# The norm ahead of the MLP: per chunk half, beside the second half of the output projection, in a region of fixed order

## The chip, the core and the metric

The kernel runs on one core of a Trainium2 chip. The metric is device time in microseconds (us) of one execution. Engines are named as the profile names them: PE (TensorE), DVE (VectorE), ACT (ScalarE), POOL (GpSimd), and SP, whose queue issues most DMAs. PE's clock has two levels here, 1.2 and 2.4 GHz; the profile gives the granted one as a share of the higher.

## The reference, cut to what matters

```python
    mixed = jnp.concatenate([rmsnorm(attn, g_attn_out), rmsnorm(ssm, g_ssm_out)], axis=-1) @ w_out
    h = x + mixed
    hn = rmsnorm(h, g_mlp)
    h = h + jnp.square(jax.nn.relu(hn @ w_up)) @ w_down
```

There are 1088 token columns, a model width of 1024 and an MLP width of 4096. All is in 32-bit floats; the kernel gets there by splitting each operand of a product in a high and a low part and adding three products (high by high, high by low, low by high).

## The kernel before

**Layout.** Tokens lie along columns. The 1088 columns fall into two halves `t` (544 each), and each half into two chunks `c` of `NC` = 272. `hp[c][t]` (128 x 8 x 272) holds `h` of one such quarter, in eight groups of 128 rows.

**The second half of the output projection.** `wo_part(w, zh, zl, c, t, mp)` makes two of the eight row groups of one quarter by 24 matmuls of 272 columns and adds them onto `hp[c][t]` on DVE (L1511). The attention half of `w_out` runs first; the state-space half (`wo2`) is the loop of 16 parts ahead of `Top, rrs = {}, {}`: four parts `mp` for each quarter, in the order c0t0, c0t1, c1t0, c1t1.

**The norm.** `norm_sq` squares a quarter on ACT and adds the squares up on POOL (t = 0) or DVE (t = 1); `mlp_norm(c)` begins when both quarters of a chunk are done. It sums over partitions by eight matmuls with a column of ones (L1622), makes the reciprocal root in a chain of small DVE and ACT operations (`rsqrt_col`, L84 to L92), spreads it over the partitions by eight transposes (L1633), copies the rows to SBUF, and multiplies `hp` by gain and rows (L333, 128x272 each).

**The MLP's operands.** The first product, `hn @ w_up`, is done block by block with seven products instead of eight (Strassen and Winograd's scheme). Its seven operands of a chunk, `Hop[c][0..6]` (`ho` in the rows), are blocks of `hn` or sums and differences of them (`nt`), each split in high (ACT cast, L1670) and low (DVE subtraction, L51), 128x1088 each. On the weights' side `w_stream` loads a set of 512 KB blocks (`wr`), forms the sums (`ws`, DVE, 128x512) and splits each of the seven in high (ACT, L1595) and low (POOL, L51): tiles `wl`, six buffers.

**The order of products.** `up_pair(0)` does the sets 0 and 1 for chunk 0 alone (14 products of 12 matmuls; results in `hold`), so that PE has work while chunk 1 is normed. Then `up_set(b)` does set 2 to 15 for both chunks (14 products each), `up_pair(1)` does sets 0 and 1 for chunk 1, and the second product of the MLP follows. The names on PE's rows are `Xp`, `Yp`, `Zp` in a pair and `X`, `Y`, `Z` in a set; a set makes X, Y, X, Y, X, Z, X.

**What sets the order.** `mlp_norm` is a generator: `pump()` runs each live one to its next `yield` after every part or product. The order in which the code then stands is not the order on the engines: outside of `tc.manual_schedule()` the framework's scheduler orders each engine's instructions by its own estimate and by which buffer is free. Inside it, an engine keeps the order of the code. Each engine works through its own queue in that order, and an instruction that waits holds up all behind it. PSUM gives four buffers of 128 x 2 x 512 (`psa`); pages (`pg`, 15 of them) hold `hp`, the projection's operands and weights, and `ho`.

Of the kernel before, what the change touches and what calls it, by code (L numbers as in the profile page):

```python
# [22 lines left out]
EPS = 1e-6  # L23
# [6 lines left out]
def tile_hybrid_step(ctx: ExitStack, tc: tile.TileContext, I: dict, O: dict):  # L30
# [1467 lines left out]
    def wo_part(w, zh, zl_, c, t, mp):  # L1498

        c0 = NH * t + NC * c  # L1500
        ps = psa(f"pw{c}{t}_{mp}")
        for k in range(2):
            m_ = slice(128 * (2 * mp + k), 128 * (2 * mp + k) + 128)
            o = ps[:, k, :NC]
            for kt in range(4):
                rh, rl = zh[kt // 2][:, kt % 2, c0:c0 + NC], zl_[kt // 2][:, kt % 2, c0:c0 + NC]
                pe.matmul(o, lhsT=w[kt][0][:, m_], rhs=rh, start=(kt == 0), stop=False)  # L1507
                pe.matmul(o, lhsT=w[kt][0][:, m_], rhs=rl, start=False, stop=False)  # L1508
                pe.matmul(o, lhsT=w[kt][1][:, m_], rhs=rh, start=False, stop=(kt == 3))  # L1509
        o = hp[c][t][:, 2 * mp:2 * mp + 2]  # L1510
        dve.tensor_tensor(o, ps[:, :, :NC], o, op=ALU.add)  # L1511
        pump()
# [3 lines left out]
    wo_part(wo, ah, al, *order[0])  # L1516
# [24 lines left out]
    for c, t, mp in order[1:2]:  # L1541
        wo_part(wo, ah, al, c, t, mp)
    live.append(ssm_norm())
    for c, t, mp in order[2:]:
        wo_part(wo, ah, al, c, t, mp)
# [14 lines left out]
    def w_stream():  # L1560
# [54 lines left out]
    Hop = [[], []]  # L1615

    def sums(sq, name):

        ps = psb(name + "s")
        for t in range(2):  # L1620
            for j in range(4):
                pe.matmul(ps[:TT, 4 * t + j:4 * t + j + 1], lhsT=sq[:, t, TT * j:TT * j + TT], rhs=ones,  # L1622
                          start=True, stop=True)
        return ps

    def inv_rows(ps, name):

        rsqrt_col(col[0][:TT], ps[:TT, 0:8], 1024, [t[:TT] for t in col[1:3]])
        yield
        pr_ = psa(name + "r")  # L1630
        for t in range(2):
            for j in range(4):
                pe.transpose(pr_[:, t, TT * j:TT * j + TT], col[0][:TT, 4 * t + j:4 * t + j + 1].to_broadcast([TT, 128]),  # L1633
                             ident[:TT, :TT])
        rows = rq([128, 2, NC], name + "rows")
        act.copy(rows, pr_[:, :, :NC])
        return rows

    nsq = []

    def norm_sq(c, t, mp, part):

        if mp == 1:
            part[c, t] = rq([128, 4, NC], f"ns{c}{t}a")
            act.activation(part[c, t], hp[c][t][:, 0:4], AF.Square)
        elif mp == 3:
            s1, s2 = part[c, t], rq([128, 4, NC], f"ns{c}{t}b")
            act.activation(s2, hp[c][t][:, 4:8], AF.Square)
            e = dve if t else pool
            e.tensor_tensor(s1, s1, s2, op=ALU.add)  # L1650
            e.tensor_tensor(s1[:, 0:2], s1[:, 0:2], s1[:, 2:4], op=ALU.add)
            e.tensor_tensor(nsq[c][:, t], s1[:, 0], s1[:, 1], op=ALU.add)
            c0 = NH * t + NC * c
            nc.sync.dma_start(hs[:, :, c0:c0 + NC], hp[c][t])

    def mlp_norm(c):

        sq = nsq[c]
        rows = yield from inv_rows(sums(sq, f"n{c}"), f"n{c}")
        yield  # L1660

        def quarter(k, t):
            for kt in range(4 * k, 4 * k + 4):
                z = hp[c][t][:, kt]
                stt(z, z, g_ml[:, kt:kt + 1], rows[:, t], ALU.mult, ALU.mult)
            return hp[c][t][:, 4 * k:4 * k + 4]

        def operand(src, le):
            h = pg([128, 2, 4, NC], f"ho{c}_{len(Hop[c])}", F32R)
            act.copy(h[:, 0], src)  # L1670
            lo_sub(le, h[:, 1], src, f(h[:, 0]))
            Hop[c].append(h)

        b11 = quarter(0, 0)
        operand(b11, dve)
        yield
        b12 = quarter(0, 1)
        t1 = rq([128, 4, NC], f"nt1{c}")
        dve.tensor_tensor(t1, b12, b11, op=ALU.subtract)
        operand(t1, dve)  # L1680
        yield
        b22 = quarter(1, 1)
        t2 = rq([128, 4, NC], f"nt2{c}")
        dve.tensor_tensor(t2, b22, t1, op=ALU.subtract)
        operand(t2, dve)
        yield
        t3 = rq([128, 4, NC], f"nt3{c}")
        dve.tensor_tensor(t3, b22, b12, op=ALU.subtract)
        operand(b22, dve)
        yield  # L1690
        operand(t3, dve)
        yield
        b21 = quarter(1, 0)
        operand(b21, dve)
        yield
        dve.tensor_tensor(t2, b21, t2, op=ALU.subtract)
        operand(t2, dve)
# [13 lines left out]
    def relu2(z):  # L1711
        stt(z, z, 0.0, z, ALU.max, ALU.mult)

    def up_evac(i, o, z):

        if i in (0, 1, 2):
            act.copy(z(*((0, 0), (1, 1), (1, 0))[i]), o)
        elif i in (3, 4, 5):
            z = z(*((1, 0), (1, 1), (0, 0))[i - 3])
            dve.tensor_tensor(z, o, z, op=ALU.add)  # L1720
            relu2(z)
        else:
# [21 lines left out]

    for _ in range(4):
        ahead.append(next(wst))
    part = {}
    for c in range(2):
        nsq.append(rq([128, 2, NC], f"nsq{c}"))
        for t in range(2):  # L1750
            for mp in range(4):
                wo_part(wo2, sh, sl, c, t, mp)
                norm_sq(c, t, mp, part)
        live.append(mlp_norm(c))
# [28 lines left out]

    def up_pair(c):

        rt = [hold[:, s_] if c == 0 else rq([128, 2, 2, NC], f"rb{s_}") for s_ in range(2)]
        made = {}
        for i, x in enumerate(SEQ):
# [3 lines left out]
            for s_ in range(2):  # L1792
                w = w_next()
                while len(Hop[c]) <= i:
                    pump()
                o = made[x][:, s_, :NC]
                up_product(w, o, i, c, first)
                up_evac(i, o, lambda k, q: rt[s_][:, k, q])
            pump()
            if c == 1 and 1 <= i < 5:  # L1800
# [3 lines left out]
    def up_set(b):  # L1804
        rt = [rq([128, 2, NH], f"r{x}{b}") for x in "ab"]
        made = {}
        for i, x in enumerate(SEQ):
            w = w_next()
# [3 lines left out]
            for c in range(2):  # L1812
                while len(Hop[c]) <= i:
                    pump()
                up_product(w, made[x][:, c, :NC], i, c, first)
            up_evac(i, made[x][:, :, :NC], lambda k, q: rt[k][:, q].rearrange("p (c n) -> p c n", c=2))
            pump()
# [3 lines left out]
    up_pair(0)  # L1821
    for b in range(2, 16):
# [40 lines left out]
    for g in range(8):  # L1863
        for jp in range(2):
# [3 lines left out]
            for i, x in enumerate(SEQ):  # L1868
                w = w_next()
# [19 lines left out]
    ws = [w_next() for _ in range(7)]  # L1889
# [322 lines left out]
```

## Time and profile before

| | us |
|---|---|
| runs: 1386.16, 1387.05, 1392.28; median | 1387.05 |
| the profiled execution, its own time | 1385.12 |
| its span, first to last instruction | 1382.9 |
| PE busy in it | 1299.2 (94%) |
| DVE, POOL, ACT busy | 1039.1, 685.6, 662.5 |

PE is busy for 94% of the span. Its clock is granted in full nearly everywhere (0.980 in the mean). In the 40 slices of the page, each 34.6 us long, slices 19 to 21, where the projection's second half ends and the MLP begins, are among those with PE busy for less than nine tenths.

### The profile page before, as it was taken

How to read it: one execution, taken by the hardware profiler on the slowest of the kernel's cores; microseconds unless marked ns; L12 is line 12 of the kernel's file. 1: busy time of each engine (PE TensorE's matmuls, PEld its weight loads, DVE VectorE, ACT ScalarE, POOL GpSimd, SP SyncE). 2: the span in 40 equal slices, each digit the busy share in tenths (PEclk: the TensorE clock that was granted, in tenths of full speed). 3: DMA queues.
4: the chain of work that ended last, by engine and by line, in shares of the span. 5: the costliest groups of instructions: out<-in, count | busy, mean ns of one | idle time of the engine just before them, and what ended most of it. 6: DMA issues, size and time to landing. Idle time of an engine off the chain costs nothing.

```text
span 1382.9 us, 24883 instructions
## 1 busy us (share of the span) xinstructions
PE 1299.2 (94%) x9552; PEld 1258.4 (91%) x9552; DVE 1039.1 (75%) x1658; ACT 662.5 (48%) x1325; POOL 685.6 (50%) x646
## 2 busy tenths in 40 slices
PE   7999998989999997998599999999989999999996
PEld 6999997978888887998599999999979999999996
DVE  8679779876888766659877557565699778888756
ACT  6576677655788762224232232332446333343333
POOL 3647656341535426243465455455547455453554
PEclk9999999999999999999899999999999999999998
DMA  5111111210233234132233353342668445654103
GB/s 220 64 41 41 35 35 36 77 48 8 48 76 78 69 94 128 31 126 69 71 129 128 135 175 115 147 167 104 207 235 295 134 154 161 202 163 140 62 1 130
DMA packets 81286, 151.38 MB, mean 109 GB/s; under 512 B 10128, under 2 KB 28816, under 8 KB 81168
## 3 DMA queue, kind: packets, MB, share of 16 engines
q1 hardware_dynamic: 76464, 144.78, 32.7%
q10 hardware_dynamic: 4704, 5.01, 1.1%
q8 instruction: 76, 1.25, 0.4%
q14 instruction: 42, 0.34, 0.1%
HBM read 98.66 MB, written 41.40 MB: 101 GB/s over the span
## 4 chain that ended last, share of the span: by engine, by line
PE 46%; DVE 9%; POOL 3%; issue 2%; DMA 2%; ACT 1%; SPq 0%; DVEq 0%; POOLq 0%; ACTq 0%
PE dX L1701 4%; PE dX L1702 4%; PE dX L1703 4%; PE X L1701 3%; PE X L1703 3%; PE X L1702 3%; POOL wl L51 2%; PE dY L1701 2%; PE dY L1703 2%; PE dY L1702 2%; PE pw L1507 2%; PE pw L1508 2%; PE pw L1509 2%; PE Y L1701 2%; PE Y L1703 2%
## 5 line engine op out<-in xcount | busy, mean ns | idle before, releaser
L51 POOL TENSOR_TENSOR wl<-ws,wl 128x512 fp32r<-128x512 f32 x101 | 163.4, 1619 | 237.0 <-ACT wl L1595 234.8
L51 POOL TENSOR_TENSOR wl<-wr,wl 128x512 fp32r<-128x512 f32 x135 | 210.7, 1569 | 105.6 <-ACT wl L1595 102.4
L1595 ACT CAST wl<-ws 128x512 fp32r<-128x512 f32 x102 | 63.3, 621 | 194.0 <-DVE ws L1583 85.6
L1701 PE MATMUL dX<-to,wl 128*128 128x272 f32 x512 | 149.3, 292 | 2.1 <-DVE q L1858 1.4
L1702 PE MATMUL dX<-to,wl 128*128 128x272 f32 x512 | 148.1, 289 | 0.0
L1703 PE MATMUL dX<-to,wl 128*128 128x272 f32 x512 | 147.6, 289 | 0.0
L1703 PE MATMUL X<-ho,wl 128*128 128x272 f32 x448 | 129.5, 290 | 5.4 <-POOL wl L51 5.4
L1701 PE MATMUL X<-ho,wl 128*128 128x272 f32 x448 | 128.4, 291 | 2.0 <-DVE rb L1720 2.0
L1702 PE MATMUL X<-ho,wl 128*128 128x272 f32 x448 | 128.8, 289 | 0.0
L1595 ACT CAST wl<-wr 128x512 fp32r<-128x512 f32 x136 | 83.9, 620 | 90.4 <-PE dX L1703 31.6
L1581 DVE TENSOR_TENSOR ws<-wr,wr 128x512 f32<-128x512 f32 x34 | 30.8, 905 | 103.2 <-DMA wr<-in_w_up_dram 79.2
L1701 PEld LDWEIGHTS dX<-to,wl 128*128 128x128 f32 x512 | 97.2, 190 | 3.1 <-issue 1.1
L1702 PEld LDWEIGHTS dX<-to,wl 128*128 128x128 f32 x512 | 97.1, 190 | 0.0
L1703 PEld LDWEIGHTS dX<-to,wl 128*128 128x128 f32 x512 | 96.9, 189 | 0.0
L1858 DVE TENSOR_TENSOR q<-dX,q 128x544 f32<-128x544 f32 x108 | 76.0, 717 | 27.8 <-PE dX L1703 27.6
L1703 PEld LDWEIGHTS X<-ho,wl 128*128 128x128 f32 x448 | 84.6, 189 | 5.9 <-POOL wl L51 5.9
L1701 PEld LDWEIGHTS X<-ho,wl 128*128 128x128 f32 x448 | 83.9, 189 | 2.4 <-DVE rb L1720 2.4
L1702 PEld LDWEIGHTS X<-ho,wl 128*128 128x128 f32 x448 | 84.6, 189 | 0.0
L51 DVE TENSOR_TENSOR to<-rr,to 128x1088 fp32r<-128x1088 f32 x56 | 83.5, 1496 | 1.3 <-ACT to L1776 1.3
L1701 PE MATMUL dY<-to,wl 128*128 128x272 f32 x256 | 74.7, 292 | 4.7 <-DVE rb L333 3.1
L1703 PE MATMUL dY<-to,wl 128*128 128x272 f32 x256 | 74.5, 291 | 1.6 <-POOL wl L51 1.6
L1702 PE MATMUL dY<-to,wl 128*128 128x272 f32 x256 | 74.3, 290 | 0.0
(707 smaller groups left out, 4653.6 us busy)
## 6 DMA issues: line engine op xcount, KB each, us to landing
rr<-rd SPq DMA_DIRECT2D x56, 544.0 KB, 5.0
wr<-in_w_up_dram SPq DMA_DIRECT2D x36, 512.0 KB, 4.4
wr<-in_w_dn_dram SPq DMA_DIRECT2D x32, 512.0 KB, 4.7
rd<-rc SPq DMA_DIRECT2D x16, 544.0 KB, 3.6
rd<-re SPq DMA_DIRECT2D x16, 544.0 KB, 3.7
rd<-ra SPq DMA_DIRECT2D x28, 272.0 KB, 3.1
xw<-in_x_dram SPq DMA_DIRECT2D x8, 544.0 KB, 6.8
hp<-in_x_dram ACTq DMA_DIRECT2D x4, 1088.0 KB, 6.1
```

Source lines behind the costliest of these rows:

```text
L51: eng.tensor_tensor(out, src, hi, op=ALU.subtract)
L1507: pe.matmul(o, lhsT=w[kt][0][:, m_], rhs=rh, start=(kt == 0), stop=False)
L1508: pe.matmul(o, lhsT=w[kt][0][:, m_], rhs=rl, start=False, stop=False)
L1509: pe.matmul(o, lhsT=w[kt][1][:, m_], rhs=rh, start=False, stop=(kt == 3))
L1581: dve.tensor_tensor(s_, a21, a22, op=ALU.add)
L1595: act.copy(w[:, 0], src)
L1701: pe.matmul(o, lhsT=lh, rhs=rh, start=first, stop=False, skip_group_check=True)
L1702: pe.matmul(o, lhsT=lh, rhs=rl, start=False, stop=False, skip_group_check=True)
L1703: pe.matmul(o, lhsT=ll, rhs=rh, start=False, stop=last, skip_group_check=True)
L1858: dve.tensor_tensor(z, o[:, :, :NC], z, op=ALU.add)
```

## The change

The 16 parts of the projection's second half, the norm, sets 0 and 1 for chunk 0 and the whole of set 2 now stand in one `tc.manual_schedule()` region. `mlp_norm(c, t)` is a generator for one quarter: it begins after the third part of its own quarter and works beside the parts that follow. Its sums and transposes are four and four; the rows stay in PSUM and the multiplications read them there; all sums of squares are on DVE; each operand's low part is put off to the next step (`later`). `up_pair(0)` is replaced by `up_first`: chunk 0 goes through sets 0 and 1 by eight plain products for each set (24 matmuls for each of eight weight tiles, 192 in all, where the pair had 168), which need the four plain blocks of chunk 0 (`ho0_0`, `ho0_7`, `ho0_5`, `ho0_3`) and eight plain weight tiles, whose low parts are made on DVE (not POOL) and need no sums. Evacuation of `up_first` and of set 2's squared ReLU is on ACT. The operands 1, 2, 4 and 6 of chunk 0 are first needed in set 2. Before and behind the region the order on the engines is that of before but for a few instructions.

```diff
+        load(0)
+        yield
         for j, ns in enumerate(SETS):
             load(j)
+            if j == 0:
+                for n, raw in zip(ns, raws[j]):
+                    for q in range(4):
+                        w = wo4([128, 2, 512], f"wl{j}_{n}_{q}", F32R)
+                        act.copy(w[:, 0], raw[q % 2][:, q // 2])
+                        lo_sub(dve, w[:, 1], raw[q % 2][:, q // 2], f(w[:, 0]))
+                        if n == ns[0] and q == 3:
+                            load(1)
+                        yield w
+                del raws[j]
+                continue
...
+    def mlp_norm(c, t):
+        x, hc = hp[c][t], Hop[c]
+        s1, s2 = (rq([128, 4, NC], f"ns{c}{t}{k}") for k in range(2))
+        act.activation(s1, x[:, 0:4], AF.Square)
+        yield
+        yield
+        act.activation(s2, x[:, 4:8], AF.Square)
...
+        dve.tensor_tensor(s1, s1, s2, op=ALU.add)
+        dve.tensor_tensor(s1[:, 0:2], s1[:, 0:2], s1[:, 2:4], op=ALU.add)
+        dve.tensor_tensor(s1[:, 0], s1[:, 0], s1[:, 1], op=ALU.add)
+        yield
+        for _ in range(c + (c and t)):
+            yield
+        ps = psa(f"n{c}{t}")
+        for j in range(4):
+            pe.matmul(ps[:TT, 1, j:j + 1], lhsT=s1[:, 0, TT * j:TT * j + TT], rhs=ones, start=True, stop=True)
...
+        for j in range(4):
+            pe.transpose(ps[:, 0, TT * j:TT * j + TT], col[c][:TT, 4 * t + j:4 * t + j + 1].to_broadcast([TT, 128]),
+                         ident[:TT, :TT])
+        yield
+        def scale(k):
             for kt in range(4 * k, 4 * k + 4):
+                z = x[:, kt]
+                stt(z, z, g_ml[:, kt:kt + 1], ps[:, 0, :NC], ALU.mult, ALU.mult)
...
+    def up_first():
...
+                o = psa(f"d{s_}{r}")
+                for k in range(2):
+                    w = ahead.pop(0)
+                    for t in range(2):
+                        up_product(w, o[:, t, :NC], ((0, 7), (5, 3))[k][t], 0, k == 0)
+                    flush()
+                    w_next()
+                    step()
...
+    with tc.manual_schedule():
+        next(wst)
+        for n, (c, t) in enumerate(parts):
+            for mp in range(4):
+                late.append(wo_part(wo2, sh, sl, c, t, mp))
+                if len(late) > 1:
+                    late.pop(0)()
+                if mp == 2:
+                    live.append(mlp_norm(c, t))
+                step()
+                if 4 * n + mp in WAT:
+                    w_next()
+        up_first()
+        up_set(2, True)
+    for b in range(3, 16):
+        up_set(b)
```

On PE, where the norm's sums (`n1s`) and transposes (`n1r`) of chunk 1 stood before, among the products of the first pair:

```order
L1703 MATMUL Xp0_7489<-ho0_0_7308,wl0_0_0_6958 128x272
L1622 MATMUL n1s_7528<-ones_67,nsq1_7197 68x1 x4
L1701 MATMUL Yp0_7543<-ho0_1_7343,wl0_0_1_6965 128x272
...
L1703 MATMUL Yp0_7543<-ho0_3_7415,wl0_1_3_7562 128x272
L1633 MATMUL n1r_7578<-ident_64,col0_6944 128x68 x8
L1701 MATMUL Zp0_7720<-ho0_5_7479,wl0_0_5_7634 128x272
```

And PE now, for the two quarters of chunk 1 (`n10`, `n11`; `pw11_3` is the last part of the projection, `d00` to `d11` are `up_first`):

```order
L1668 MATMUL n10_7449<-ones_67,ns100_7322 68x1 x4
L1507 MATMUL pw11_3_7463<-sh0_6421,wo4_6785 128x272
...
L1680 MATMUL n10_7449<-ident_64,col1_6945 128x68 x4
L1737 MATMUL d00_7496<-ho0_0_7273,wl0_0_0_7133 128x272
...
L1668 MATMUL n11_7639<-ones_67,ns110_7460 68x1 x4
L1737 MATMUL d10_7650<-ho0_0_7273,wl0_1_0_7286 128x272
...
L1680 MATMUL n11_7639<-ident_64,col1_6945 128x68 x4
L1737 MATMUL d11_7722<-ho0_0_7273,wl0_1_2_7561 128x272
```

The sums of chunk 1's first quarter have moved ahead of the projection's last part, its transposes behind it, and those of the second quarter stand 96 and 144 matmuls into `up_first`; set 2 follows `d11`.

On DVE, ahead of chunk 1's sums before (`ns11a`, `nsq1` are the sums of squares of the last quarter, `ho0` the operands of chunk 0):

```order
L51 TENSOR_TENSOR ho0_2_7384<-nt20_7382,ho0_2_7384 128x1088
L51 TENSOR_TENSOR ho0_3_7415<-hp01_6134,ho0_3_7415 128x1088
L1696 TENSOR_TENSOR nt20_7382<-hp00_6133,nt20_7382 128x1088
L51 TENSOR_TENSOR ho0_4_7446<-nt30_7413,ho0_4_7446 128x1088
L51 TENSOR_TENSOR ho0_5_7479<-hp00_6133,ho0_5_7479 128x1088
L1650 TENSOR_TENSOR ns11a_7418<-ns11a_7418,ns11b_7482 128x1088
L51 TENSOR_TENSOR ho0_6_7525<-nt20_7382,ho0_6_7525 128x1088
L1651 TENSOR_TENSOR ns11a_7418<-ns11a_7418 128x544
L1652 TENSOR_TENSOR nsq1_7197<-ns11a_7418 128x272
```

And DVE now, the end of the chain from the last quarter's reciprocal root (L1670 to L333) to `ho1_1`, the second operand of chunk 1:

```order
L1728 TENSOR_TENSOR nt01_7446<-hp01_6134 128x1088
L51 TENSOR_TENSOR ho1_0_7603<-hp10_6135,ho1_0_7603 128x1088
L1731 TENSOR_TENSOR nt02_7447<-hp00_6133,nt02_7447 128x1088
L1670 TENSOR_SCALAR n11_7639<-n11_7639 68x4
...
L51 TENSOR_TENSOR ho0_4_7634<-nt01_7446,ho0_4_7634 128x1088
L51 TENSOR_TENSOR ho1_5_7637<-hp10_6135,ho1_5_7637 128x1088
...
L333 SCALAR_TENSOR_TENSOR hp11_6136<-hp11_6136,gains_65,n11_7639 128x272 x4
L1713 TENSOR_TENSOR nt11_7809<-hp11_6136,hp10_6135 128x1088
L1722 TENSOR_TENSOR nt12_7810<-hp11_6136,nt11_7809 128x1088
L51 TENSOR_TENSOR ho1_1_7824<-nt11_7809,ho1_1_7824 128x1088
```

The sums of squares no longer stand behind the operands of chunk 0; instead two of chunk 0's operands and one difference stand between chunk 1's norm and `ho1_1`.

## Rows read from the trace of the kernel before

**Rows 1.** The page, section 1: busy time of each engine, share, instructions.

```profile
PE 1299.2 (94%) x9552; PEld 1258.4 (91%) x9552; DVE 1039.1 (75%) x1658; ACT 662.5 (48%) x1325; POOL 685.6 (50%) x646
```

**Rows 2.** PE's timeline: the first wo2 matmul, and the first Y of set 4.

```profile
591.28 0.29 PE L1507 MATMUL pw<-sh,wo 128*128 128x272 f32 x1
...
737.60 0.29 PE L1701 MATMUL Y<-ho,wl 128*128 128x272 f32 x1
```

**Rows 3.** Windows: length, busy us (count) of PE, PEld, DVE, ACT, POOL; granted clock.

```profile
591.28:643.30 52.02, 50.13 (x410) 49.85 (x409) 36.59 (x52) 14.69 (x18) 20.89 (x13) 1.00 0.32 106
643.30:682.80 39.50, 27.02 (x195) 25.60 (x194) 35.55 (x44) 15.43 (x25) 18.71 (x11) 0.87 0.24 82
682.80:709.30 26.50, 21.53 (x155) 20.87 (x153) 23.98 (x28) 12.96 (x19) 18.78 (x8) 0.94 0.21 72
709.30:737.60 28.30, 26.34 (x207) 26.11 (x207) 20.32 (x23) 8.57 (x15) 17.01 (x11) 1.00 0.36 128
737.60:758.77 21.17, 21.17 (x170) 21.17 (x169) 13.45 (x17) 6.30 (x11) 10.54 (x8) 1.00 0.42 147
```

**Rows 4.** What PE waited for from 591 to 738: total, times, longest us.

```profile
PE n1s L1622 <- DVE nsq L1652: 6.6, 1, 6.6
PE X L1703 <- POOL wl L51: 5.4, 2, 4.3
PE Xp L1701 <- DVE hold L1720: 3.1, 2, 2.4
PE n0r L1633 <- DVE col L92: 1.6, 1, 1.6
```

**Rows 5.** Windows of 5 us behind or around three waits of PE.

```profile
665.00:670.00 5.00, 5.00 (x34) 5.00 (x33) 2.23 (x5) 1.84 (x4) 1.52 (x2) 0.67 0.00 0
675.00:680.00 5.00, 2.57 (x19) 2.15 (x18) 5.00 (x12) 0.00 (x0) 0.71 (x1) 1.00 0.03 9
690.00:695.00 5.00, 3.49 (x18) 3.49 (x19) 3.85 (x4) 1.70 (x4) 3.54 (x3) 0.72 0.16 56
```

**Rows 6.** DVE's timeline: a split and a difference alone; a split beside POOL.

```profile
633.43 1.28 DVE L51 TENSOR_TENSOR ho<-hp,ho 128x1088 fp32r<-128x1088 f32 x1
634.63 1.28 DVE L1679 TENSOR_TENSOR nt<-hp,hp 128x1088 f32<-128x1088 f32 x1
...
653.52 2.38 DVE L51 TENSOR_TENSOR ho<-hp,ho 128x1088 fp32r<-128x1088 f32 x1
```

**Rows 7.** POOL's timeline: a weight split alone, and one beside DVE's splits.

```profile
600.51 1.29 POOL L51 TENSOR_TENSOR wl<-wr,wl 128x512 fp32r<-128x512 f32 x1 [3.09 <-ACT wl L1595]
653.31 1.44 POOL L51 TENSOR_TENSOR wl<-wr,wl 128x512 fp32r<-128x512 f32 x1 [0.86 <-ACT wl L1595]
```

**Rows 8.** Groups of instructions, last 53 us: DVE's multiplications by PSUM rows, POOL's.

```profile
L333 DVE SCALAR_TENSOR_TENSOR q<-q,gains,fin 128x272 f32<-128x272 f32 x12 | 5.7, 488 | 0.9 <-ACT frows L2083 0.9
...
L1968 POOL TENSOR_TENSOR q<-q,frows 128x544 f32<-128x544 f32 x7 | 9.3, 1346 | 9.9 <-ACT frows L2025 7.0 <-ACT frows L2083 1.7 <-ACT frows L2098 1.2
```

**Rows 9.** DVE's timeline: the norm's sums, and first and last of the root's chain.

```profile
618.30 1.29 DVE L1650 TENSOR_TENSOR ns01a<-ns01a,ns01b 128x1088 f32<-128x1088 f32 x1 [1.18 <-ACT ns01b L1648]
620.14 0.71 DVE L1651 TENSOR_TENSOR ns01a<-ns01a 128x544 f32<-128x544 f32 x1
620.89 0.44 DVE L1652 TENSOR_TENSOR nsq<-ns01a 128x272 f32<-128x272 f32 x1
...
623.48 0.15 DVE L84 TENSOR_SCALAR col<-n0s 68x8 f32<-68x8 f32 x1
...
624.53 0.16 DVE L92 SCALAR_TENSOR_TENSOR col<-col,col 68x8 f32<-68x8 f32 x1
```

**Rows 10.** ACT's groups of instructions, 591 to 738: casts of weights and of operands.

```profile
L1595 ACT CAST wl<-wr 128x512 fp32r<-128x512 f32 x19 | 11.7, 621 | 11.0 <-DMA wr<-in_w_up_dram 7.6 <-PE Yp L1703 1.4 <-POOL wl L51 1.4
L1670 ACT CAST ho<-hp 128x1088 fp32r<-128x1088 f32 x6 | 6.6, 1100 | 1.3 <-DVE hp L333 1.3
```

**Rows 11.** PE's timeline: eight transposes of the norm.

```profile
624.84 0.66 PE L1633 MATMUL n0r<-ident,col 68*128 68x68 f32 x8 [1.61 <-DVE col L92]
```

More of the change, by code (lines that the diff above doesn't have):

```diff
@@ L1510, in wo_part, with add @@
         o = hp[c][t][:, 2 * mp:2 * mp + 2]
-        dve.tensor_tensor(o, ps[:, :, :NC], o, op=ALU.add)
-        pump()
+        def add():
+            dve.tensor_tensor(o, ps[:, :, :NC], o, op=ALU.add)
+        return add
     parts = [(c, t) for c in range(2) for t in range(2)]
     order = [(c, t, mp) for mp in range(4) for c, t in parts]
-    wo_part(wo, ah, al, *order[0])
+    wo_part(wo, ah, al, *order[0])()
     pp_.close()
@@ L1606, in w_next, with w_take @@
     def w_next():
+        ahead.extend([x for x in [next(wst, None)] if x is not None])
+    def w_take():
         w = ahead.pop(0)
-        ahead.extend([x for x in [next(wst, None)] if x is not None])
+        w_next()
         return w
+    WAT = (5, 6, 7, 8, 9)
     hs = dram.tile([128, 8, NT], F32, name="hs")
@@ L1614, in tile_hybrid_step @@
     col = [ph3.tile([128, 8], F32, name=f"col{j}") for j in range(4)]
[L1615 to L1628, printed above, removed]
-        yield
[L1630 to L1637, printed above, removed]
@@ L1656, in mlp_norm @@
-    def mlp_norm(c):
-        sq = nsq[c]
-        rows = yield from inv_rows(sums(sq, f"n{c}"), f"n{c}")
-        yield
-        def quarter(k, t):
-            for kt in range(4 * k, 4 * k + 4):
[L1664 to L1669, printed above, removed]
-            act.copy(h[:, 0], src)
[L1671 to L1675, printed above, removed]
-        yield
-        b12 = quarter(0, 1)
-        t1 = rq([128, 4, NC], f"nt1{c}")
+    Hop = [{}, {}]
@@ L1679, in mlp_norm @@
         dve.tensor_tensor(t1, b12, b11, op=ALU.subtract)
-        operand(t1, dve)
         yield
[L1682 to L1685, printed above, removed]
+        if c == 0:
+            operand(3, b22)
+            dve.tensor_tensor(t2, b22, t1, op=ALU.subtract)
+            yield
+            operand(1, t1)
+        else:
+            operand(1, t1)
+            dve.tensor_tensor(t2, b22, t1, op=ALU.subtract)
@@ L1697, in mlp_norm @@
-        operand(t2, dve)
+        operand(6, t2)
     def three(o, l, r, first, last):
@@ L1742, in up_sums @@
         nc.sync.dma_start(out[:, 4:7:2], re)
[L1745 to L1754, printed above, removed]
     Top, rrs = {}, {}
@@ L1782, in tile_hybrid_step, with flush, squared @@
     hold = pg([128, 2, 2, 2, NC], "hold")
+    late = []
+    def flush():
+        for z in late:
+            z()
+        late.clear()
+    def up_first():
+        def squared(z, o):
+            act.activation(z, o, AF.Relu)
+            act.activation(z, z, AF.Square)
+        for s_ in range(2):
+            for r in range(2):
+                o = psa(f"d{s_}{r}")
[6 more added lines that the diff above has]
+                    step()
+                late.append(lambda s_=s_, r=r, o=o: squared(hold[:, s_, :, r], o[:, :, :NC]))
     def up_pair(c):
-        rt = [hold[:, s_] if c == 0 else rq([128, 2, 2, NC], f"rb{s_}") for s_ in range(2)]
+        rt = [rq([128, 2, 2, NC], f"rb{s_}") for s_ in range(2)]
         made = {}
@@ L1886, in tile_hybrid_step @@
         pump()
-    ws = [w_next() for _ in range(7)]
+    ws = [w_take() for _ in range(7)]
     sqp = rq([128, 2, 2, NC], "sqp")
```

117 lines of the change are left out of this document (75 added, 42 removed).

## The prediction

> **What bounds the kernel now.** The page first: PE is busy for 94% of the span [rows 1], so what can be won is time in which PE waits or runs slowly. The windows show where. From 737.6 us a set of 168 matmuls takes 21.17 us without a gap, 0.126 us for each [rows 3]; from 643.3 to 682.8 PE is busy 27.0 of 39.5 us at a clock of 0.87, and the two windows behind that are short too.
>
> How much is lost there is counted, not summed from waits. The second half of the projection begins at 591.28 and set 4's first Y at 737.60 [rows 2], 146.3 us. The order of instructions has 912 matmuls of 272 columns between them (384 for the projection, 168 each for the pair and for sets 2 and 3, and 24 of set 4), hence 114.9 us. The norm's 16 column sums and 16 transposes (32 small matmuls) are an estimated 2 us, from 0.66 us for eight transposes [rows 11] with sums taken alike and some overlap. That leaves 29.4 us of loss. The waits name most of it: the norm's sums for chunk 1 wait 6.6 us for DVE, a product of set 2 waits 4.3 us for a weight split on POOL, others wait for evacuations [rows 4]. The rest is restarts and clock: behind the 6.6 us wait PE runs at 0.67, in the window of the 4.3 us one at 0.72, while around a wait of 2.4 us it stays at 1.00 [rows 5]; 0.67 lies between the two levels, 1.2 GHz and 2.4 GHz. The cause is DVE: it is busy 35.6 of 39.5 us in that window [rows 3], with chunk 0's splits ahead of chunk 1's sums of squares in its queue.
>
> **The change, part by part.** Behind set 4's first Y the order on all engines is that of before but for a few swaps, so what is won up to there is the whole of it. I set t = 0 at 591.28.
>
> *PE's work.* `up_first` takes 192 matmuls where the pair took 168: +24, +3.0 us, surely on the path. Now 936 matmuls, 117.9 us, and the same 32 small ones, 2: 119.9 us with no loss. That would be 26.4 us less than 146.3.
>
> *The norm beside the projection.* A part takes 24 x 0.126 = 3.03 us. Each of the first three quarters does its sums, root and multiplications while PE has other parts. For c0t0: its last add can run at 12.2, ACT squares until 14.1, DVE's three sums take 2.3 us less small overlaps (1.29, 0.71, 0.44) [rows 9] to 16.4; PE comes to its sums at 18.2. The root's chain takes 1.2 us (623.48 to 624.69) [rows 9], done at 20; PE comes to the transposes at 21.4. For c0t1 the same reckoning gives sums at 29.5 against 30.8 and transposes 32.4 against 34; for c1t0 43 against 46.4 and 47.9 against 49.6. So these steps cost PE nothing, but the margins are 1.2 to 3 us. A wider wait there has nothing to hide it, since PE's order is now fixed. The weight splits added on DVE, eight of 128x512, are an estimated 0.6 us each, by the 128x544 sum's 0.71 [rows 9] less what successive instructions overlap; five of them lie in this stretch, where DVE has room.
>
> *The change to `up_first`.* The projection ends at 49.6, transposes take 0.25, `d00` begins at 49.85. Its last operand, `ho0_3`, needs a page that comes free only when the last part is through: ACT casts it at 49.8 (1.10 us), then a weight tile (0.62, mean of the casts) [rows 10]; DVE splits that tile and `ho0_3` (0.6, 1.2; a split alone is 1.20 from start to next start [rows 6]), done at 53.4. PE needs it at 49.85 + 36 x 0.126 = 54.4. Hidden, by 1 us.
>
> *Set 2, where I expect the loss.* Set 2 begins at 49.85 + 192 x 0.126 + 0.45 (c1t1's sums and transposes) = 74.5. After 36 matmuls, at 79.0, it needs `ho1_1`. From 53.4 on, DVE has no idle time ahead of that: 16 multiplications of 128x272 at 0.42 (0.49 less overlap [rows 8]) 6.7; sums 2.3; seven splits and four differences of 128x1088 at 1.20 [rows 6] 13.2; six sums and splits of 128x512 at 0.6, 3.6; the root 1.2. Together 27.0, so `ho1_1` is there at 80.4 if nothing slows DVE. But now POOL makes set 2's weight splits beside it. A split of 128x1088 that took 1.28 alone took 2.38 beside POOL [rows 6, 7], 1.1 us more. Six weight splits fall in the stretch; by the order three of them lie beside multiplications with rows in PSUM, and such multiplications took 488 ns while POOL worked at its own 1346 ns ones [rows 8], no longer than the others. Three lie beside splits or differences: 3 x 1.1 = 3.3. So `ho1_1` comes at about 83.5, and PE waits 4.5 us. Bounds: 1.4 (POOL costs nothing) and 9.1 (all six cost POOL's 1.29 us [rows 7] in full).
>
> The Trainium skill ("SBUF — State Buffer", Who interferes with whom) says that a DVE instruction with two SBUF inputs and a GpSimd instruction that reads SBUF exclude each other, the second blocked until the first ends, and that one with a single SBUF input doesn't take part. The trace agrees on both kinds (2.38 against 1.28 us, and 488 ns). By that rule's full block the three would cost 3 x 1.29 = 3.9 us, 0.6 more than the row gives. It speaks against the change, which keeps set 2's splits on POOL while DVE is full.
>
> *Behind that.* The operands after `ho1_1` come 2 to 4 us apart and PE uses one pair in 3.03 us: they keep up, by 0.5 to 1 us. Clock: a wait of 4.5 us lies beside the 4.3 us one, whose window lost (1 - 0.72) x 5 = 1.4 us; I take 1.5, bounds 0 (as at 2.4 us) and 2.2 (0.67 for 5 us and some more behind the 6.6 us wait). Restarts of one or two waits: 0.3. In the order a sum of set 4's weights stands on DVE ahead of `ho1_6` and of set 2's evacuation, and waits for its load; PE needs `ho1_6` some 6 us later, so it is hidden; if that load is late by more, set 3 waits. I take 0.5 for set 3, bounds 0 and 2.0: its window before, 28.3 us, had PE busy 26.3 [rows 3].
>
> *Sum.* 119.9 + 4.5 + 1.5 + 0.3 + 0.5 = 126.7 against 146.3: 19.6 us less. The profiled execution took 1385.12 us of its own, 2.2 more than its span, so 1365.5; the median of the runs lies 1.9 above that execution, which gives **1367.5 us**.
>
> **Rivals.** *No wait at all.* If DVE gets through faster, all four losses vanish: 26.4 us, 1360.7. For it: half of POOL's splits meet PSUM operands, and the rest may fall in DVE's gaps. Against: even with POOL at no cost the sum leaves 1.4 us.
>
> *A second wait follows.* Every POOL split costs in full (9.1), the clock 2.2, set 3 its 2.0: 119.9 + 13.6 = 133.5, 12.8 us less; with one more wait of 3 us and its clock loss (`ho1_3` and `ho1_4` are only 0.5 to 1 us ahead of PE) 8 us less: 1374 to 1379.
>
> *The loss only moves.* Before, the scheduler put products between the norm and its use; now PE stops at each sum and transpose that is late. If DVE runs 20% over my durations, the margins of 1.2 to 3 us are gone in three quarters; three waits of 3 us with 1.5 of clock each (13.5), on top of the 6.8 above, leave 6 us: 1381, within noise.
>
> *Slower: the clock.* The fixed region holds 744 matmuls of 272 columns. At the lower level one costs 0.227 us at the least (272 columns at 1.2 GHz, where 0.126 is the row at the higher). If waits of 3 to 6 us follow one another and PE stays at that level between them, each matmul loses 0.10 us, and beyond 260 of them the 26.4 us are spent. Set 2 and `up_first` alone, 360, would give 36 us, 10 more than before: 1397. For it: 0.67 behind the longest wait. Against: a wait of 2.4 us left the clock at 1.00, and behind the one of 6.6 us it was back within the next 5 us or so [rows 4, 5].
>
> The Trainium skill ("TensorE: Matmul & The Clock Gate", Part 1) has the half clock as the default that only sustained activity lifts; rows 5 agree, as the low clock stands behind the two long waits alone.
>
> **How the numbers follow.** My forecast, gains of 13 to 24 us: 58%. No wait: 17%. A second wait, 7 to 13 us: 14%. The loss only moves: 6%. Slower: 5%. Single runs of before lie within 0.5% of each other, about 7 us, and that is what a measurement can tell from no change. Faster by over 0.5% is 58 + 17 + 14 = 89%, within 0.5% 6%, slower 5%. The range holds the forecast's band, all of the case without a wait down to 1361, and the second wait up to 1378; beyond lie the last two cases and bits of the others. The likeliest case's own range is 1363 to 1374.
>
> **What would show it.** In the profile after: the projection's 384 matmuls in about 49 us with no wait of over 1 us; `n00`, `n01`, `n10` without waits; 192 matmuls of `up_first` in 24 to 25 us; one wait of PE on DVE's `ho1_1` in set 2, of 3 to 6 us, with a lower clock behind it; set 4's first Y near 718 us on a time axis in which the first `wo2` matmul stands at 591.3; DVE's 128x1088 splits at 1.28 until POOL's first weight split of set 2, and up to 2.4 beside such. Wrong would be: waits already among the projection's parts (then the margins failed), no wait in set 2 (POOL's share failed), or a first Y of set 4 at 718 and yet another end (then the rest did not move as one block).

## The result, and the profile after

The changed kernel took 1370.01 us (median of 4 runs, 1368.57 to 1373.97) against 1388.01 us for the kernel before (4 runs beside it, 1386.16 to 1392.28): a ratio of 0.9881, 95% interval 0.9862 to 0.9901. Faster by 1.2%, 18.0 us by the medians; the forecast of 1367.5 us was 2.5 us too low.

The page of the profiled execution, its span and its section 1:

```profile
span 1366.8 us, 24903 instructions
...
PE 1299.2 (95%) x9576; PEld 1260.1 (92%) x9576; DVE 1022.3 (75%) x1657; ACT 665.5 (49%) x1327; POOL 651.3 (48%) x626
```

24 matmuls more than in [rows 1], in the same 1299.2 us of busy PE: what went was time in which PE stood idle or ran slowly, not work. The span went from 1382.9 us to 1366.8, 16.1 less. PE's timeline at the two ends of the stretch of [rows 2], and at the points of the prediction between them:

```profile
592.99 0.29 PE L1507 MATMUL pw<-sh,wo 128*128 128x272 f32 x1
...
670.64 0.29 PE L1737 MATMUL X<-ho,wl 128*128 128x272 f32 x1
...
676.82 0.39 PE L1737 MATMUL Y<-ho,wl 128*128 128x272 f32 x1 [1.49 <-ACT ho L1691]
679.18 0.39 PE L1738 MATMUL Y<-ho,wl 128*128 128x272 f32 x1 [1.97 <-DVE ho L51]
...
721.59 0.29 PE L1737 MATMUL Y<-ho,wl 128*128 128x272 f32 x1
```

The stretch took 721.59 - 592.99 = 128.6 us where it took 146.3: 17.7 us less. Outside it the two spans differ by 1.6 us the other way. The start of the stretch alone, behind code that the kernels here hardly touch, lies between 589.1 and 596.1 us in the profiles of this study. So the experiments below are compared by this stretch first, which is one profile of each, and by the times second; each ratio is against runs of the kernel before that were taken beside it. All that PE waited for in the stretch (total, times, longest us):

```profile
PE Y L1738 <- DVE ho L51: 2.0, 1, 2.0
PE Y L1737 <- ACT ho L1691: 1.5, 1, 1.5
PE pw L1509 <- POOL wo L51: 1.3, 1, 1.3
```

The waits of [rows 4] are gone: no sum or transpose of the norm waits, and none of set 2's products for POOL. Left are the two halves of one wait for `ho1_1`, its cast on ACT and then its low part on DVE, and one wait in the projection's first part that I had not seen coming. Windows of 5 us around the wait for `ho1_1`, columns as in [rows 3]:

```profile
670.00:675.00 5.00, 5.00 (x42) 5.00 (x41) 5.00 (x10) 2.81 (x5) 2.66 (x3) 1.00 0.00 0
675.00:680.00 5.00, 1.54 (x10) 1.12 (x9) 4.97 (x4) 4.17 (x5) 3.90 (x2) 1.00 0.52 161
680.00:685.00 5.00, 5.00 (x30) 5.00 (x29) 5.00 (x4) 2.30 (x4) 2.62 (x2) 0.66 0.32 108
685.00:690.00 5.00, 5.00 (x41) 5.00 (x41) 5.00 (x6) 2.24 (x3) 1.27 (x1) 1.00 0.00 0
```

PE is busy for 1.5 us of the second window, makes its next 30 matmuls at a clock of 0.66 in the mean, and is back in the fourth. Cut finer, the clock is at its lower level (0.50, which is 1.2 GHz) from 680.0 to 683.4 and full behind it:

```profile
680.00:683.40 3.40, 3.40 (x17) 3.40 (x16) 3.40 (x3) 1.20 (x3) 1.04 (x2) 0.50 0.42 140
683.40:685.00 1.60, 1.60 (x15) 1.60 (x14) 1.60 (x2) 1.10 (x1) 1.59 (x1) 1.00 0.11 40
```

DVE is busy through all of these windows.

The stretch adds up, with PE's starts read off its timeline: 936 matmuls 117.9; the norm's four groups of sums (0.46 each) and of transposes (0.21 each) 2.7; the first part's wait 1.3; the wait for `ho1_1` 3.5; set 2's other loss 2.0 (26.7 us from start to start, less 21.17 and 3.5), most of it clock; set 3 0.1; and short gaps in the projection and `up_first`, 1.1. That is 128.6.

### The profile page after: what moved, and what is told of

Read it like the earlier page. It is cut to its first block, busy times and chain, and to the rows that moved or that the text cites. A ratio compares the mean times of both kernels' runs of the same rounds, so it can differ in the third digit from the quotient of the medians.

```text
span 1366.8 us, 24903 instructions
## 1 busy us (share of the span) xinstructions
PE 1299.2 (95%) x9576; PEld 1260.1 (92%) x9576; DVE 1022.3 (75%) x1657; ACT 665.5 (49%) x1327; POOL 651.3 (48%) x626
## 4 chain that ended last, share of the span: by engine, by line
PE 49%; DVE 8%; issue 2%; POOL 1%; ACT 1%; DMA 1%; DVEq 0%; POOLq 0%; ACTq 0%
PE X L1737 4%; PE X L1739 4%; PE X L1738 4%; PE dX L1737 4%; PE dX L1738 4%; PE dX L1739 4%; PE pw L1507 2%; PE pw L1508 2%; PE pw L1509 2%; PE Y L1738 2%; PE Y L1739 2%; PE Y L1737 2%; PE dY L1737 2%; PE dY L1738 2%; PE dY L1739 2%
## 5 line engine op out<-in xcount | busy, mean ns | idle before, releaser
L51 POOL TENSOR_TENSOR wl<-wr,wl 128x512 fp32r<-128x512 f32 x127 | 200.3, 1585 | 156.1 <-ACT wl L1613 94.0
L51 POOL TENSOR_TENSOR wl<-ws,wl 128x512 fp32r<-128x512 f32 x95 | 149.9, 1578 | 225.8 <-ACT wl L1613 225.8
L1613 ACT CAST wl<-ws 128x512 fp32r<-128x512 f32 x96 | 59.7, 622 | 191.9 <-DVE ws L1601 94.2
L1613 ACT CAST wl<-wr 128x512 fp32r<-128x512 f32 x128 | 79.0, 621 | 80.4 <-PE dX L1739 32.2
L1599 DVE TENSOR_TENSOR ws<-wr,wr 128x512 f32<-128x512 f32 x32 | 27.0, 845 | 93.6 <-DMA wr<-in_w_up_dram 71.6
L51 DVE TENSOR_TENSOR to<-rr,to 128x1088 fp32r<-128x1088 f32 x56 | 83.7, 1499 | 2.6 <-ACT to L1808 2.6
```

The lines of the kernel that those rows point to most:

```text
L51: eng.tensor_tensor(out, src, hi, op=ALU.subtract)
L1599: dve.tensor_tensor(s_, a21, a22, op=ALU.add)
L1613: act.copy(w[:, 0], src)
```

## The experiments

The first five take apart what the change joined, and price what is left; the others go after the waits that are left. The stretch always runs from the first `wo2` matmul to set 4's first Y.

**Without the fixed order.** The region is given to the scheduler.

```diff
-    with tc.manual_schedule():
+    if True:
```

> The code of the change, with its region left to the scheduler. Theory (the gain comes from when the norm's and the operands' instructions are issued, quarter by quarter; the fixed order only keeps it): the norm's sums and transposes stay within some 20 matmuls of where they stand, products that need the late weight of the projection may go behind others, so PE's 1.3 us wait on it goes, the wait for the second operand of chunk 1 stays: 1366 to 1371 us, the stretch from the first matmul of the projection's second half to set 4's first Y 126 to 129 us. Rival (the fixed order brings the gain): the stretch is nearer to the 146 us of before than to 128.6, above 1378 us.

Measured: 1381.82 us, ratio 0.9941 (0.9919 to 0.9963), stretch 592.41 to 732.07, 139.7 us. PE's waits there, and what DVE did ahead of the longest:

```profile
PE n L1668 <- DVE ns L1662: 12.8, 3, 7.5
```

```profile
659.30 1.28 DVE L1660 TENSOR_TENSOR ns<-ns,ns 128x1088 f32<-128x1088 f32 x1
661.11 1.28 DVE L1728 TENSOR_TENSOR nt<-hp 128x1088 f32<-128x1088 f32 x1
...
665.32 0.71 DVE L1661 TENSOR_TENSOR ns<-ns 128x544 f32<-128x544 f32 x1
665.95 1.28 DVE L51 TENSOR_TENSOR ho<-nt,ho 128x1088 fp32r<-128x1088 f32 x1
...
670.02 1.49 DVE L1662 TENSOR_TENSOR ns<-ns 128x272 f32<-128x272 f32 x1
```

The norm's three sums, 3.5 us of work here that PE waits for, are strung out over 12 us: the scheduler put splits and differences between them, among them chunk 0's (`nt` in the rows), which PE needs only in set 2, 94.3 us into the stretch. My theory, that the order brings little, fell. 11.1 of the 17.7 us hang on the fixed order.

**Seven products for chunk 0**, all else as changed (the fixed order and the norm by halves), except that the weight splits of sets 0 and 1 are on POOL again and set 2's products wait in the code for their operands:

```diff
-        for s_ in range(2):
-            for r in range(2):
...
+        for i, x in enumerate(SEQ):
+            first = x not in made
```

> Chunk 0 goes through sets 0 and 1 by seven products again, beside the norm per quarter and in the fixed order; weight splits on GpSimd again; 24 matmuls (3.0 us) fewer. Theory (eight products buy time for VectorE): set 2 starts 3 us earlier, VectorE has eight sums of weights more and no splits fewer in sum, 14 GpSimd splits in place of none stand beside it, so the second operand of chunk 1 comes 0 to 4 us later than now and PE waits for the first products as well: 3 to 10 us slower than the change, 1373 to 1380 us. Rival (the norm per quarter is all of it): the 3.0 us of matmuls are won, about 1367 us.

Measured: 1378.7 us, ratio 0.9925 (0.9907 to 0.9943), stretch 140.2 us.

```profile
PE Y L1727 <- ACT ho L1691: 5.4, 1, 5.4
PE Xp L1727 <- ACT hold L1747: 3.9, 2, 3.6
PE Yp L1727 <- ACT hold L1747: 2.9, 1, 2.9
```

The theory held in the time and in the wait for `ho1_1`, not in the start of set 2: it had set 2 begin 3 us earlier. The pair waits 6.8 us for evacuations (Xp and Yp behind `hold`), and set 2 begins at 83.4 us of the stretch instead of 77.7; `ho1_1` is later still, and is waited for 7.2 us (5.4 here, and 1.8 for its low part).

**The eight products alone, in the kernel before:** its own norm and scheduler, with `up_first` and the operand and split orders that it needs.

```diff
-    up_pair(0)
+    up_first()
     for b in range(2, 16):
```

> The kernel before with only the eight products: chunk 0 goes through the first two sets by eight products on undivided operands (0, 7, 5 and 3 made first), the splits of those two sets on VectorE and their evacuation on ScalarE, but the norm stays whole per chunk, behind the projection's chunk, in the scheduler's order. Theory (the norm by halves in fixed order is what takes most of the loss out; the eight products alone only shorten the time in which all seven operands must be made): the stretch stays within 5 us of before's 146.3, at 141 to 151. Rival (needing four operands instead of seven is the change's gain): the stretch falls below 135 us, near the changed kernel's 128.6.

Measured: 1377.9 us, ratio 0.9934 (0.9916 to 0.9952), stretch 589.47 to 728.18, 138.7 us. Neither range held it: the eight products alone are worth 7.6 us, more than the theory gave them, less than the rival. They end the waits for X and Xp of [rows 4] but leave the norm's:

```profile
PE n1s L1633 <- DVE nsq L1663: 6.0, 1, 6.0
PE n1r L1644 <- DVE col L92: 4.2, 1, 4.2
PE n0r L1644 <- DVE col L92: 1.6, 1, 1.6
```

So of 17.7 us the eight products alone give 7.6, the norm by halves in fixed order without them 6.1, and both without the fixed order 6.6. None of these gives half, and the first two add up to 13.7: the parts work together. The fixed order is needed, and so are the eight products. What the norm by halves is worth by itself is not shown: the fixed order with eight products and the norm still whole per chunk was not run, and in the scheduler's order the norm by halves adds nothing to the eight products (6.6 against 7.6).

**The eight products' weight splits back on POOL**, one word of the change:

```diff
-                        lo_sub(dve, w[:, 1], raw[q % 2][:, q // 2], f(w[:, 0]))
+                        lo_sub(pool, w[:, 1], raw[q % 2][:, q // 2], f(w[:, 0]))
```

> Only the low parts of the eight plain weight tiles go back from VectorE to GpSimd. Theory: VectorE is rid of 8 x 0.6 us, of which three stand where it is full, and pays about 1.1 us for each GpSimd split beside its own two-input work there: within 2 us of the change, 1368 to 1372 us. Rival (keeping GpSimd out of this stretch matters): GpSimd's splits take 2 us and more beside VectorE, weights come late, PE waits in the eight products: over 4 us slower, above 1374 us.

Measured: 1371.38 us, ratio 0.9866 (0.9842 to 0.989), stretch 129.0 us. The theory held: this part of the change is worth nothing that can be measured.

**Set 2 without POOL's splits.** The kernel leaves out the subtraction for set 2's low parts: ACT copies the block in their place.

```diff
+                    if j == 1:
+                        act.copy(w[:, 1], src)
```

> Leaves out part of the computation: the low parts of set 2's seven weight tiles are copies of the same block by ScalarE, and GpSimd has nothing to do beside the chain to chunk 1's second operand. Theory (GpSimd's share in the lateness is 3 to 4 us): splits and differences on VectorE take 1.28 us throughout, the operand comes 3 to 4 us earlier, PE's waits in set 2 (1.5 and 2.0 us) shrink below 1 us and the low clock behind them goes: 4 to 6 us faster than the change, 1364 to 1366 us. Rival (VectorE is late by its own amount of work): waits of over 2 us in set 2 stay, within 2 us of the change.

Measured: 1364.42 us, ratio 0.9828 (0.9806 to 0.9849), stretch 125.0 us. The wait for `ho1_1` falls from 3.5 us to 0.2, and the clock stays at 1.00: without POOL's work beside DVE that operand is not late. The theory held. This prices the wait; it is no way to mend it.

```profile
PE pw L1509 <- POOL wo L51: 1.3, 1, 1.3
PE X L1740 <- ACT rb L1760: 1.2, 1, 1.2
PE Y L1741 <- DVE ho L51: 0.2, 1, 0.2
```

**The wait in the first part** (late_weight). The low part of the eighth `wo` tile goes from POOL to DVE, and the first part takes the tiles in the order in which they come.

```diff
-    WHE, WLE = '02', '2357'
+    WHE, WLE = '02', '235'
...
+        if w is wo2 and (c, t, mp) == (0, 0, 0):
+            kts.sort(key=lambda x: x[1])
```

> Changed kernel with one edit at the head of the region: the low part of the eighth wo tile is made by VectorE instead of GpSimd, and the first part's products take the tiles in the order in which they come, so that the eighth's come last. Theory (the 1.3 us in which TensorE waits for that low part, which my sum lacked, is a cost of the fixed order at that place alone): the wait is gone, the stretch falls from 128.6 to 127.0 to 127.5 us, and the median by about as much. Rival (the low part's maker is not what is late, or the time comes back at set 2, where VectorE decides): some wait of 1 us or more stays in the first part, or set 2's wait grows by what the first part gained, and the stretch stays at 128 to 129.5.

Measured: 1365.63 us (1364.95 to 1369.53), ratio 0.9855 (0.9836 to 0.9875), stretch 589.97 to 718.03, 128.1 us. The 1.3 us wait is gone and set 2 begins 1.6 us earlier in the stretch, but the stretch is only 0.5 us shorter. The wait for `ho1_1` is the same 2.0 and 1.5 us; what grew is the loss to the clock behind it:

```profile
670.00:675.00 5.00, 1.50 (x9) 1.08 (x7) 4.97 (x4) 3.96 (x6) 3.59 (x2) 0.87 0.51 161
675.00:680.00 5.00, 5.00 (x24) 5.00 (x24) 5.00 (x4) 2.34 (x4) 1.98 (x2) 0.50 0.32 108
680.00:685.00 5.00, 5.00 (x39) 5.00 (x39) 5.00 (x5) 2.62 (x4) 1.26 (x2) 0.95 0.00 0
```

24 matmuls in the middle window at 0.50, where the changed kernel made 30 at 0.66. The lower level holds here from 673.65 to 680.45, twice as long as in the changed kernel, and set 2 takes 1.1 us more. Why the same wait costs more clock here is not shown. Theory and rival each have half of it: the wait was where I said, its time came back elsewhere.

**DVE's work by due time** (due_order). Chunk 1's differences, `ho1_1` and `ho1_2` go ahead of `ho0_4`, `ho0_6` and `ho1_5`, which PE needs later.

```diff
+            while c and len(go) < 2:
+                yield
             operand(5, b21)
...
-        operand(4, t1)
+        while len(go) < 1:
+            yield
+        operand(4, t1)
```

> Changed kernel with VectorE's work of the region put in order of its due time: chunk 1's differences and the low parts of ho1_1 and ho1_2 ahead of ho0_4, ho0_6 and ho1_5, which set 2 needs later. Nothing is added or left out. Theory (TensorE's 3.5 us of waiting at the head of set 2, and the low clock behind it, come from the order in which VectorE makes the operands, not from how much it has to make): ho1_1 and ho1_2 are done before TensorE comes to them, both waits fall below 0.5 us, the clock stays at 1.00 behind them, and the stretch from the first wo2 matmul to set 4's first Y falls from 128.6 to 123.5 to 125 us; median near 1366 against 1370. Rival (VectorE is full from the projection's end to set 2, so a product put forward is paid by the one put back): a wait of 2 to 4 us shows at a later product of set 2 or at the end of chunk 0's products, and the stretch stays at 127 to 129.5.

Measured: 1375.75 us, ratio 0.9926 (0.9907 to 0.9945), stretch 592.68 to 729.53, 136.9 us: 8 us worse than the changed kernel. `ho1_1` came in time and two other waits took its place.

```profile
PE X L1761 <- ACT ra L1781: 5.6, 1, 5.6
PE Y L1761 <- ACT rb L1781: 3.2, 1, 3.2
```

DVE's timeline shows the first cause, ACT's the second:

```profile
664.40 0.69 DVE L1601 TENSOR_TENSOR ws<-ws,wr 128x512 f32<-128x512 f32 x1 [2.05 <-POOL wl L51]
667.21 0.69 DVE L1603 TENSOR_TENSOR ws<-wr,ws 128x512 f32<-128x512 f32 x1 [2.11 <-POOL wl L51]
667.82 1.72 DVE L333 SCALAR_TENSOR_TENSOR hp<-hp,gains,n 128x272 f32<-128x272 f32 x4
```

```profile
678.47 1.09 ACT L1691 CAST ho<-hp 128x1088 fp32r<-128x1088 f32 x1
679.47 2.09 ACT L1691 CAST ho<-nt 128x1088 fp32r<-128x1088 f32 x2
681.47 0.60 ACT L1781 COPY ra<-X 128x544 f32<-128x544 f32 x1
```

A weight sum of set 2 is made in place and must wait until POOL has read the one before. In the changed kernel `ho0_4`, `ho1_5` and `ho0_6` fill that time; moved back, they leave DVE idle for twice 2 us with the multiplications queued behind. And they come back later as casts on ACT: `ho0_4` (one of the two at 679.47) ahead of the copy of X that PE waits for, `ho0_6` and `ho1_5` ahead of the copy of Y. The theory fell. The rival's sign came, waits at later products of set 2, at more than its price; its reason did not, for DVE stood idle and was not full.

**Both edits** (due_and_weight: due_order and late_weight together):

> Both edits: VectorE's work in order of due time, and the eighth wo tile's low part on VectorE with its products last in the first part. Theory (the two losses are apart from each other): the gains add, the stretch falls to 122 to 124 us, and the median to 1363 to 1366. Rival (starting set 2 a microsecond earlier moves TensorE nearer to VectorE's last operands): the second gain is eaten by a wait at set 2's later products, stretch 124.5 to 127.

Measured: 1377.37 us, ratio 0.9937 (0.9917 to 0.9958), stretch 134.1 us, with the waits of due_order (5.6 and 3.7 us). Neither range held it; it falls with due_order.

**Only ScalarE's copies of due_order mended** (due_order_copies): each of set 2's first three copies is issued straight behind its product.

```diff
+                    elif i < 3:
+                        up_evac(i, made[x][:, :, :NC], lambda k, q: rt[k][:, q].rearrange(
+                            "p (c n) -> p c n", c=2), held)
                     step()
```

> due_order with one edit: set 2's first three copies out of PSUM are issued on ScalarE straight behind their product instead of one step later, behind the casts. Theory (the 5.6 and 3.2 us in which TensorE waited for those copies are ScalarE's order, not its amount of work): both waits for ScalarE's copies fall below 1 us, the stretch falls from due_order's 136.9 to 128 to 132, still with waits for VectorE's low parts, since VectorE stands behind GpSimd as before. Rival (ScalarE is late because VectorE is, and the copies only show it): waits of the same sum, 7 us or more, at the casts or low parts, stretch 135 or more.

Measured: 1376.63 us, ratio 0.9901 (0.9877 to 0.9926), stretch 594.03 to 730.96, 136.9 us; waits of 3.6 (X) and 5.8 us (Y) at the same two copies. The rival held in the sum of the waits and in the stretch, though they show at the copies and not at the casts or low parts: one step earlier the copies still stood behind casts that waited for DVE.

**DVE's order mended at its cause** (scales_first), on top of late_weight: all of `n11`'s multiplications and both differences in one go, sums of set 2 in buffers of their own, `ho1_5` and `ho0_6` later, copies as in the run before.

```diff
         scale(0)
+        if c and t:
+            scale(1)
...
+            dve.tensor_tensor(t1, b12, b11, op=ALU.subtract)
+            operand(1, t1)
+            dve.tensor_tensor(t2, b22, t1, op=ALU.subtract)
...
+                        if j == 1:
+                            src = ph3.tile([128, 512], F32, name=f"ws{j}_{n}_{i}", tag="ws", bufs=2)
```

> The kernel with the eighth wo tile's low part on VectorE (late_weight) with a new order at set 2. As soon as the transposes of the last norm (n11) are made, VectorE makes all of that half's multiplications and both differences in one go; ho1_5 and ho0_6 move behind ho1_4, ho0_4 stays. Set 2's second and third weight sums go into buffers of their own, so that VectorE need not wait until GpSimd has read the sum before. Set 2's first three copies out of PSUM stand on ScalarE straight behind their product, ahead of the casts that come later. Nothing is left out. Theory (due_order lost 8 us because VectorE stood 2 times 2 us behind GpSimd ahead of those multiplications, and because the copy of X stood behind five casts on ScalarE; without these two the operands come in time): no wait of TensorE over 1 us at set 2, the clock stays up, the stretch falls from late_weight's 128.1 to 122.5 to 125 us, and the median from 1365.6 to 1361 to 1363.5. Rival (VectorE has more to make between the projection's end and set 2's last products than there is time for, whatever the order): a wait of 2 us or more at ho1_1 or at a later product stays, stretch 126.5 to 130.

Measured: 1369.16 us, ratio 0.986 (0.9838 to 0.9883), stretch 592.5 to 722.98, 130.5 us, 2.4 more than late_weight's. No operand is late any more, but the copies still are, 3.2 and 2.6 us (X, Y). The stretch lies in neither range. DVE's part of the theory was right; ACT's order was not yet mended.

**ACT's order mended too** (copies_early): `ho1_3` and what follows are cast behind the copies, the copy of X ahead of the last evacuation of `up_first`.

```diff
+            yield
+            yield
+            operand(3, b22)
...
-                    flush()
+                    if i or c:
...
+                        flush()
```

> scales_first with ScalarE's order mended: set 2's copies out of PSUM now stand ahead of the casts of ho1_3 and those after them, and the copy of X ahead of the last eight-product evacuation; VectorE's order is kept but for set 3's first weight sum, which comes ahead of ho1_6 and ho0_6. Nothing is left out. Theory (in scales_first all operands came in time, and its 3.2 and 2.6 us of waiting are copies behind casts that wait for VectorE): no wait of TensorE over 1 us from the first part to set 4, the clock at 1.00, stretch from 130.5 to 122 to 125 us, median 1360 to 1364. Rival (there is more to do on VectorE and ScalarE between the projection's end and set 2's end than they have time for; each order only names another victim): a wait of 2 us or more shows at some other instruction of set 2 or 3, stretch 126.5 or more.

Measured: 1366.43 us (1363.83 to 1368.19), ratio 0.9846 (0.9823 to 0.9869), stretch 593.54 to 717.92, 124.4 us, 4.2 less than the changed kernel's. All of PE's waits:

```profile
PE Y L1771 <- ACT rb L1791: 1.0, 1, 1.0
PE X L1771 <- ACT rb L1784: 0.7, 1, 0.7
PE X L1771 <- ACT ra L1791: 0.5, 1, 0.5
```

The theory held in the stretch and the waits, and missed in the time (1360 to 1364 expected). The times do not tell this kernel from the others so clearly: the interval overlaps those of the changed kernel (0.9881) and of late_weight (0.9855). Against the kernel before, this one and late_weight are the best of those that leave nothing out; which of the two is better stays open.

## Why the prediction was right, step by step

**The count of loss, and the place.** Right. 936 matmuls at 0.126 us and the stretch's two ends carried the forecast: 17.7 us won there of 19.6 forecast, and set 4 to set 5 takes 21.17 us as in [rows 3]. (Of the slices of the page named ahead of the prediction, 19 and 20 are below nine tenths, 21 is not; the count does not use them.) The 1.9 us that the stretch lacks are a balance: the wait in the first part (1.3), small matmuls (0.7), short gaps (1.1) and set 2's other loss (0.2) came on top, the wait for `ho1_1` (1.0) and set 3 (0.4) were smaller than forecast.

**The norm beside the projection costs PE nothing.** Right, all of its waits vanished. The small matmuls were sized at 2 us and took 2.7.

**PE's order in the projection.** Here a term was missing, the sum had none for it: 1.3 us. The wait was hidden before, because the scheduler let PE take other products until POOL had split the eighth `wo` tile; the fixed order takes that cover away. The forecast asked this of every norm step and not of the projection's own operands. The run without the fixed order has no such wait. In late_weight it went with the split's move and the new order of the products together, which were not tried apart, and its price was not 1.3 us in the end. The prediction's "no wait of over 1 us" among the 384 matmuls was wrong by this one, though it was not the norm's margins that failed. With it, 0.6 us more of small matmuls and 0.8 of short gaps, the projection ended at 52.3 instead of 49.6, and set 2 began at 77.7 instead of 74.5.

**`ho0_3` hidden by 1 us.** Right: done at 648.0, needed at 650.1, hidden by 2.

**The wait for `ho1_1`: 4.5 us, bounds 1.4 and 9.1.** Right in kind and place, 3.5 us in size; that the size came so near is in part luck. Both ends of the wait moved: PE came for `ho1_1` at 82.2 instead of 79.0, for the reasons just given, and DVE had it at 86.1 instead of 83.5 (by the prediction's own terms 80.4 + 3.3 = 83.7). POOL's share was forecast at 3.3; without POOL's splits the wait fell by 3.3, from 3.5 to 0.2. It is made of other pieces than I gave, though. DVE's timeline, from POOL's second split of set 2 on:

```profile
663.78 2.37 DVE L51 TENSOR_TENSOR ho<-hp,ho 128x1088 fp32r<-128x1088 f32 x1
...
669.14 0.69 DVE L1603 TENSOR_TENSOR ws<-wr,ws 128x512 f32<-128x512 f32 x1 [1.18 <-POOL wl L51]
669.75 1.72 DVE L333 SCALAR_TENSOR_TENSOR hp<-hp,gains,n 128x272 f32<-128x272 f32 x4
...
673.96 1.68 DVE L1713 TENSOR_TENSOR nt<-hp,hp 128x1088 f32<-128x1088 f32 x1
675.67 2.25 DVE L1722 TENSOR_TENSOR nt<-hp,nt 128x1088 f32<-128x1088 f32 x1
677.85 3.58 DVE L51 TENSOR_TENSOR ho<-nt,ho 128x1088 fp32r<-128x1088 f32 x2
```

One split pays the 1.1 us of [rows 6] in full, the differences 0.4 and 1.0, and 1.2 us is a wait in the queue until POOL has read a sum, which no term had; that is 3.7 together. Multiplications by PSUM rows take 1.72 us for four beside POOL, as expected from [rows 8].

**Clock 1.5, restarts 0.3, set 3 0.5.** Set 2 lost 2.0 us beyond its wait, against 1.8; set 3 lost 0.1. Of the 2.0 the clock took 1.5, as forecast: at the lower level PE's 15 matmuls from 680.06 to 683.44 took 3.38 us, 0.225 each where they take 0.126 at the higher, close to the 0.227 of the prediction's last rival. The 0.5 that is left stands against 0.3 for restarts, which had no row behind it.

**The rivals.** No wait at all, and a second wait, didn't come. "The loss only moves" was given 6%; its sums and transposes were never late. In the experiments the loss did move, by another way than that rival's: due_order, due_and_weight, due_order_copies and scales_first each turned DVE's late operand into ACT's late copy, because DVE, ACT and PE each run a fixed queue and one put-off cast holds the next copy. copies_early shows that this was order: with both queues mended no wait over 1.0 us is left.

## What to carry to other kernels

Putting a region in fixed order takes away a scheduler's bad choices (here splits ahead of a norm's sums, 11 us) and its good ones (other products while a weight is late, 1.3 us). So ask of every operand in the region, not only of the new ones, when it comes and what hid it before. A product put forward in one engine's queue has to be followed through the other engines' queues: its cast, its buffer's reader and the copies behind them. And a wait may be worth more or less than its length: 1.3 us removed at the start gave 0.5, because the clock behind the next wait stayed low for longer.

## What the runs showed of the hardware that I had not expected

POOL can be the one that waits, for long. In the changed kernel its first split for set 2 took 6.54 us, while DVE ran five instructions with two SBUF inputs one after another at their usual pace:

```profile
655.58 6.54 POOL L51 TENSOR_TENSOR wl<-wr,wl 128x512 fp32r<-128x512 f32 x1 [59.77 <-DVE hp L333]
```

```profile
655.47 0.69 DVE L51 TENSOR_TENSOR wl<-wr,wl 128x512 fp32r<-128x512 f32 x1
656.07 1.29 DVE L51 TENSOR_TENSOR ho<-nt,ho 128x1088 fp32r<-128x1088 f32 x1
...
659.68 1.29 DVE L1731 TENSOR_TENSOR nt<-hp,nt 128x1088 f32<-128x1088 f32 x1
```

The last of them ends at 660.97, and POOL ends 1.15 us later, at 662.12. A split alone takes 1.29 us [rows 7], so nearly all of its work was done after DVE's run, and all five DVE instructions went ahead of it. The kernel before has one like it: 5.83 us at 685.63. It is not always so. The next split was let in between two DVE instructions that follow each other as closely:

```profile
662.58 1.28 DVE L51 TENSOR_TENSOR ho<-nt,ho 128x1088 fp32r<-128x1088 f32 x1
663.78 2.37 DVE L51 TENSOR_TENSOR ho<-hp,ho 128x1088 fp32r<-128x1088 f32 x1
```

```profile
663.39 1.61 POOL L51 TENSOR_TENSOR wl<-ws,wl 128x512 fp32r<-128x512 f32 x1 [1.28 <-ACT wl L1613]
```

It ends at 665.00, and the DVE split at 663.78 ends 1.15 us behind it. The Trainium skill ("SBUF — State Buffer", Who interferes with whom) has whoever issues first holding the shared ports for the whole instruction. The second case agrees; in the first, four DVE instructions that began behind POOL's went ahead of it, and why is not shown. So beside POOL a DVE instruction may cost 1.1 us more (2.37) or nothing (1.29), and the forecast's three times 1.1 was right as a sum only.
